# Finer steps in the last tile of two output projections, and the placing of the norms' sums and broadcasts

## The chip, the cores and the metric

The kernel runs on one core of one Trainium2 chip. The metric is the device time of one execution in microseconds (us), as the median of several runs. One execution was profiled; all rows shown here come from that one.

## The reference

Two layers of a decoder trunk are run for 1024 prompt tokens and 8 sample tokens, 1032 columns in all. Each layer normalises the residual, runs its mixer, adds the mixer's output projection to the residual, and then adds an embedding that is gated by a second normalised copy of the residual:

```python
for i in range(DEPTH):                       # DEPTH = 2
    hn = rmsnorm(h, norm_mix[i])
    if i % N_MIXERS == 0:
        y, S = hgrn2_mixer(hn, s_hgrn[j], w_in_a[j], lbs[j], gnorm_a[j], w_out_a[j])
    else:
        y, vt = chunk_mlp_mixer(hn, w_in_b[j], ln_v_g[j], ln_v_b[j], w_spatial[j], b_spatial[j], w_out_b[j])
    h = h + y                                # the output projection is the last step of the mixer
    gate = jax.nn.sigmoid(rmsnorm(h, norm_ple[i]) @ w_ple_gate[i])
    h = h + gate * (p[i] @ w_ple_proj[i])
```

The change concerns the place where `h = h + y` ends and `rmsnorm(h, norm_ple[i]) @ w_ple_gate[i]` begins. It is passed twice, once in each layer.

## The kernel before

Features lie on the 128 partitions, tokens along the free axis. The 1032 tokens are cut into three column groups c = 0, 1, 2 of 384, 384 and 264. The 1024 features of the residual are eight row tiles m = 0 to 7 (`hr[c][m]`, printed as h). Every matrix product is done as three products of split halves, high by high, high by low, low by high (`mm3`, lines 219 to 221), so a weight tile exists as whi (ScalarE's copy, line 146) and wlo (VectorE's difference, line 147), and an activation as bh and bl in the same way (lines 214 and 215; bl of odd k on VectorE, of even k on GpSimd).

`out_phase` is an output projection. For each row tile m it runs over the column groups; each takes 16 steps of k, so 48 products, and then `add` adds the result to h and squares it for the norm's sum (`ssq`, `sql`). For m = 7 `add` calls `done(c)`, which starts the norm of column group c as a generator (`norm_proc`).

A norm of a column group has these parts: its sum over the partitions on TensorE (`pss`, line 269: products with one column), `rms_e` on VectorE (line 272), the power -0.5 on GpSimd (`rsq`, line 228), the broadcast back over the partitions on TensorE (`pbc`, line 280), and then for each of eight k: `tmp` on VectorE (line 293), bh on ScalarE, bl on VectorE or GpSimd.

After m = 7 comes `ple`, the gate's projection. Its first `pair` runs two row tiles, g0 and g1, side by side: g0 of column group 0, g1 of column group 0, g0 of column group 1, and so on, each 24 products of a normalised column group with that tile's weights. So each of g0 and g1 has its own whi and wlo, split ahead of use, and at most two weight tiles are held at a time.

The order on TensorE is the order in which the program is written out. What runs beside the main loop is placed by `Ticks`: a spawned generator is resumed at a later tick, and `norm_proc` waits `d[0]` ticks before its sum and `d[1]` ticks before its broadcast. A generator takes its first step at the tick after it was spawned. The delays of both output projections' norms are in `NDEL[0]`, one pair for each column group. Before the change a tick falls after every 12 products, in `out_half` (at k % 4 == 3) and in `proj` (at k == 3 and at the end of a group). The other engines' queues are ordered by a scheduler from the instructions' priorities and the place at which they were written; once the order is fixed each engine takes its queue from front to back.

Of the kernel before, what the change touches and what calls it, by code (L numbers as in the profile page):

```python
# [19 lines left out]
KT = D // P  # L20
# [16 lines left out]
DL = 4  # L37
KB = 1
SDEL = ((6, 3), (6, 2), (4, 2))
NDEL = (((1, 2), (1, 3), (2, 2)), ((2, 2), (2, 4), (3, 3)))  # L40
OFF = (0, 384, 768)
W = (384, 384, 264)
NT = (3, 3, 2)
# [37 lines left out]
def trunk_kernel(ctx, tc, xT, st, pT, nrm, wina, lbl, gna, wouta, winb, lng, lnb, lngr, lnbr,  # L81
# [7 lines left out]
    def pool(stack, name, bufs=1, **kw):  # L89
        return stack.enter_context(tc.tile_pool(name=name, bufs=bufs, reuse_waits="tile", **kw))  # L90
# [71 lines left out]
    def load(n, wait=False):  # L162
        if n >= len(order) or n in loaded or wait and order[n][0] == "B":
            return
        if order[n][0] == "B":
            loaded[n] = load_unit(order[n][1])
            return
        if n not in staged:
            fetch_weights(n)
        stg = staged.pop(n)  # L170
        with tc.high_priority(offset=PRI if order[n][:2] == ("p", 1) or order[n][0] == "b" else 0):
            loaded[n] = split_weights(stg, 1024, PLAIN, wp)
# [29 lines left out]
    def take(*key):  # L202
        n = taken[0]
        assert order[n] == key, (order[n], key)
        load(n)
        load(n + 1, key[0] == "b")
        taken[0] += 1
        return loaded[n]


    last, rest = {}, {}

    def split(hi, lo, src, eng=V):
        last["split"] = A.copy(hi, src)  # L214
        last["lo"] = eng.tensor_tensor(lo, src, hi.bitcast(F32), ALU.subtract)  # L215

    def mm3(ps, wh, wl, xh, xl, first, last, more=False):

        PE.matmul(ps, wh, xh, start=first, stop=False, skip_group_check=more)  # L219
        PE.matmul(ps, wh, xl, start=False, stop=False, skip_group_check=more)  # L220
        PE.matmul(ps, wl, xh, start=False, stop=last, skip_group_check=more)  # L221

    def blk(t, j):
        return t[:, j * P:(j + 1) * P]
# [73 lines left out]
    def proj(wt, xh, xl, c):  # L298

        wh, wl = wt  # L300
        ps = pp.tile([P, 512], F32, name="ps_proj", tag="mm", bufs=3)
        for k in range(KT):
            mm3(ps[:, :W[c]], blk(wh, k), blk(wl, k), xh[:, k, :], xl[:, k, :], k == 0, k == KT - 1)
            if k == 3:
                tk.tick()
        return ps

# [64 lines left out]
    def stage2(tp, bufs):  # L372
        return lambda w: tp.tile([P, 2, 384], F32, name="zstg", bufs=bufs)[:, :, :w]

    def one(tile):
        return lambda w: tile()[:, :w].rearrange("p (k t) -> p k t", k=1)
# [5 lines left out]
    def out_half(ps, wt, zt, c, hf):  # L382
        for k in range(8):
            k0 = max(q for cc, q in zt if cc == c and q <= 8 * hf + k)
            zh, zl = (x[:, 8 * hf + k - k0, :] for x in zt[c, k0][:2])
            mm3(ps[:, :W[c]], blk(wt[0], k), blk(wt[1], k), zh, zl,
                hf == 0 and k == 0, hf == 1 and k == 7)
            if k % 4 == 3:
                yield 2

    def new_zt():
# [475 lines left out]
    def out_phase(key, zt, ssq, first, done, pre, parts, late, fill=None):  # L867

        with ExitStack() as s:
            st = stage2(pool(s, "zstg"), 3)  # L870
            zp = pool(s, "oz")

            def load_h(m):
                if m < KT:
                    src = xT[:, m] if first else hd[m]
                    with tc.issue_after(last["zt"].ins):
                        for c in CH:
                            nc.sync.dma_start(hr[c][m], src[:, OFF[c]:OFF[c] + W[c]])

            for c, k0, nk in parts:  # L880
                zt[c, k0] = (zp.tile([P, nk, W[c]], F32R, name=f"zh{c}_{k0}"),
                             zp.tile([P, nk, W[c]], F32R, name=f"zl{c}_{k0}"), nk)
            if fill:

                to = itertools.cycle([hr[c][m] for c in (2, 0) for m in range(4)])
                more = load_zt(zt, late[0], one(lambda: next(to)), 1, 8)
                todo = load_zt(zt, late[1], st, 2, 3)
                for gen, n in ((more, 8), (todo, 3)):
                    for _ in range(n):
                        next(gen)  # L890
                for _ in fill:
                    tk.tick()
                for _ in range(8):
                    next(more)
                run(todo)
                run(more)
            else:
                run(load_zt(zt, late, st, tie=False))
            for m in range(4):
                load_h(m)  # L900

            def bank():
                return pp.tile([P, 512], F32, name="ps_o", tag="mm", bufs=3)

            def half(ps, wt, c, hf):
                for _ in out_half(ps, wt, zt, c, hf):
                    tk.tick()

            def add(m, c, ps):
                with tc.high_priority(offset=PRI if m == KT - 1 else 0):  # L910
                    V.tensor_tensor(hr[c][m], hr[c][m], ps[:, :W[c]], ALU.add)  # L911
                accum_sq(sp, ssq[c], hr[c][m], m == 0, m == KT - 1, W[c])
                if m == KT - 1:
                    done(c)


            wt = pre["w"] if pre else take(key, 0, 0)
            for c in CH:
                if c not in pre:
                    pre[c] = bank()  # L920
                    half(pre[c], wt, c, 0)
            wt = take(key, 1, 0)
            pre1 = [pp.tile([P, 384], F32, name="ps_o1", tag=t, bufs=1) for t in ("pA", "po", "pt")]
            for c in CH:
                half(pre1[c], wt, c, 0)
            for m, pm in ((0, pre), (1, pre1)):
                wt = take(key, m, 1)
                for c in CH:
                    half(pm[c], wt, c, 1)
                    add(m, c, pm[c])  # L930
            for m in range(2, KT):
                wts = [take(key, m, hf) for hf in range(2)]
                load_h(m + 2)
                for c in CH:
                    ps = bank()
                    for hf in range(2):
                        half(ps, wts[hf], c, hf)
                    add(m, c, ps)

    def ple(l, ep, hh, hl, ssq, done, mid=None):  # L940
        def group(m, c, wg, pj):
            w = W[c]
            pg = proj(wg, hh[c], hl[c], c)
            gt = sp.tile([P, 384], F32, name="tmp", bufs=4)
            with tc.high_priority(offset=PRI if m >= KT - 2 else 0):
                A.activation(gt[:, :w], pg[:, :w], AF.Sigmoid)
                V.tensor_tensor(gt[:, :w], gt[:, :w], pj[:, OFF[c]:OFF[c] + w], ALU.mult)
                V.tensor_tensor(hr[c][m], hr[c][m], gt[:, :w], ALU.add)
            accum_sq(sp, ssq[c], hr[c][m], m == 0, m == KT - 1, w)
            if l == 0:  # L950
                nc.sync.dma_start(hd[m][:, OFF[c]:OFF[c] + w], hr[c][m])
            tk.tick()

        def start(m):
            pj = ep.tile([P, T], F32, name="pj", bufs=2)
            nc.sync.dma_start(pj, ppd[l][m])
            return take("g", l, m), pj

        def pair(m):
            a, b = start(m), start(m + 1)  # L960
            for c in CH:
                group(m, c, *a)
                group(m + 1, c, *b)
                if m == KT - 2:
                    done(c)

        pair(0)
        for m in range(2, KT - 2):
            if m == 3 and mid:
                mid()  # L970
            a = start(m)
            for c in CH:
                group(m, c, *a)
        pair(KT - 2)

    def norm_spawn(c, ssq, gi, act, d):
# [3 lines left out]
    act = new_act()  # L980
    out_phase("oa", zt, ssq, True, lambda c: norm_spawn(c, ssq, 1, act, NDEL[0]), pre,
              [(c, 8, 8) for c in CH], [(c, 8) for c in CH])
# [35 lines left out]
    with ExitStack() as sG:  # L1018
# [3 lines left out]
        with ExitStack() as s:  # L1022
# [7 lines left out]

            ple(0, ep, act[0], act[1], ssq2, lambda c: tk.spawn(norm_rows(c, ssq2, 2, hn, NDEL[1][c])), mid)
            for i, _ in enumerate(pple(1, ph, pl, 0, places([(pq, "pple_t", 8)]))):
# [250 lines left out]
    for g in range(8):  # L1283
# [15 lines left out]
        else:  # L1299
# [17 lines left out]
            def first():  # L1317
# [8 lines left out]
    act3 = new_act()  # L1326
    out_phase("ob", zt, ssq3, False, lambda c: norm_spawn(c, ssq3, 3, act3, NDEL[0]), {},
              [(1, 12, 4), (2, 0, 8)], [[(2, 0), (2, 8)], [(0, 8), (1, 8), (1, 12)]], pple(1, ph, pl, 1, lambda c, mm: hr[c][4 + mm]))
# [106 lines left out]
```

## Time and profile before

| | |
|---|---|
| median of 3 runs | 1916.89 us (1912.62, 1916.89, 1918.22) |
| the profiled execution | 1914.28 us, of which 1912.4 us from first to last instruction |
| TensorE (PE) busy | 1882.9 us, 98% of the span |
| VectorE (DVE) busy | 1156.3 us, 60% |
| ScalarE (ACT) busy | 800.1 us, 42% |
| GpSimd (POOL) busy | 432.8 us, 23% |
| mean granted TensorE clock | 0.993 of full speed |

In rows of a timeline the first number is the start in us from the span's beginning, the second the duration, then engine, line, operation, tiles (out<-in), shape and count. Durations of products overlap, since they are pipelined; the distance from start to start tells the pace. A bracket names the engine's idle time just before and what ended it. The first output projection ends near 948 us, the second near 1802 us.

### The profile page before, as it was taken

Reading aid. Unit: us, or ns where it says so; the run is one execution under the profiler, and the core shown is the slowest. Engines: PE = TensorE matmul, PEld = TensorE weight load, DVE = VectorE, ACT = ScalarE, POOL = GpSimd, SP = SyncE. Lnnn points to the kernel's source line nnn. Section 1 sums busy time; section 2 is a strip of 40 time slices with the busy share of each in tenths; the row PEclk is TensorE's granted clock in tenths of the full one; section 3 lists DMA queues with packets and bytes.
Section 4 is the critical chain, followed back from the end, with each engine's and each line's share of the span. In section 5 each row is a group of like instructions: output and inputs, shape, how many; then the busy total and the mean of one; then the engine's idle time right before and its main releaser. Section 6 shows DMA issues by size and latency. Waiting matters only on the chain.

```text
span 1912.4 us, 33713 instructions
## 1 busy us (share of the span) xinstructions
PE 1882.9 (98%) x13250; PEld 1856.2 (97%) x13250; DVE 1156.3 (60%) x2610; ACT 800.1 (42%) x1711; POOL 432.8 (23%) x441
## 2 busy tenths in 40 slices
PE   9999999999999999999999999999999999999997
PEld 8999999999999998999999999999999999999997
DVE  5967676766767677411465755577777776311455
ACT  6463544444454546311244544434434335311342
POOL 4110000000010001011233332345445451011321
PEclk8999999999999999999999999999999999999998
DMA  6231323222231326711243343323333236611123
GB/s 214 76 117 61 118 72 103 78 81 78 92 99 60 111 69 191 251 49 51 76 143 117 109 145 99 90 81 106 124 114 106 97 108 197 222 45 45 67 89 111
DMA packets 124302, 203.76 MB, mean 107 GB/s; under 512 B 11568, under 2 KB 97264, under 8 KB 123120
## 3 DMA queue, kind: packets, MB, share of 16 engines
q1 hardware_dynamic: 124144, 201.61, 32.2%
q8 instruction: 104, 1.70, 0.4%
q14 instruction: 54, 0.44, 0.1%
HBM read 148.75 MB, written 52.82 MB: 105 GB/s over the span
## 4 chain that ended last, share of the span: by engine, by line
PE 90%; DVE 5%; DMA 2%; POOL 1%; ACT 1%; issue 1%; SPq 0%; DVEq 0%; ACTq 0%; POOLq 0%
PE ps_proj L219 18%; PE ps_proj L221 18%; PE ps_proj L220 18%; PE ps_o L219 6%; PE ps_o L220 6%; PE ps_o L221 6%; PE ps_d L221 1%; PE ps_d L219 1%; PE ps_d L220 1%; PE psp L1255 1%; PE pC L672 1%; PE pt_o L718 1%; PE p L638 1%; PE pt_g L1061 1%; PE pss L269 1%
## 5 line engine op out<-in xcount | busy, mean ns | idle before, releaser
L219 PE MATMUL ps_proj<-bh,whi 128*128 128x384 f32 (+1 forms) x2160 | 695.1, 322 | 2.1 <-ACT pple_t L338 1.6
L221 PE MATMUL ps_proj<-bh,wlo 128*128 128x384 f32 (+1 forms) x2160 | 679.9, 315 | 0.5 <-DVE wlo L147 0.5
L220 PE MATMUL ps_proj<-bl,whi 128*128 128x384 f32 (+1 forms) x2160 | 678.8, 314 | 1.4 <-POOL bl L215 1.4
L219 PEld LDWEIGHTS ps_proj<-bh,whi 128*128 128x128 f32 x2160 | 407.4, 189 | 3.6 <-ACT pple_t L338 1.7
L220 PEld LDWEIGHTS ps_proj<-bl,whi 128*128 128x128 f32 x2160 | 407.8, 189 | 2.6 <-POOL bl L215 2.6
L221 PEld LDWEIGHTS ps_proj<-bh,wlo 128*128 128x128 f32 x2160 | 406.5, 188 | 1.7 <-DVE wlo L147 1.7
L147 DVE TENSOR_TENSOR wlo<-wstg,whi 128x1024 fp32r<-128x1024 f32 x148 | 184.8, 1249 | 147.4 <-ACT whi L146 146.2
L146 ACT CAST whi<-wstg 128x1024 fp32r<-128x1024 f32 x148 | 155.0, 1048 | 155.2 <-PE ps_proj L220 104.1
L255 POOL TENSOR_TENSOR ssq<-ssq,tmp 128x384 f32<-128x384 f32 (+1 forms) x72 | 76.3, 1060 | 406.7 <-ACT tmp L254 359.9
L911 DVE TENSOR_TENSOR h<-h,ps_o 128x384 f32<-128x384 f32 (+1 forms) x48 | 24.6, 512 | 192.4 <-PE ps_o L221 190.9
L254 ACT ACTIVATE tmp<-h 128x384 f32<-128x384 f32 (+1 forms) x72 | 35.3, 491 | 219.3 <-DVE h L911 168.9
L219 PE MATMUL ps_o<-bh,whi 128*128 128x384 f32 (+1 forms) x384 | 122.1, 318 | 0.0
L220 PE MATMUL ps_o<-bl,whi 128*128 128x384 f32 (+1 forms) x384 | 121.8, 317 | 0.0
L221 PE MATMUL ps_o<-bh,wlo 128*128 128x384 f32 (+1 forms) x384 | 121.8, 317 | 0.0
L146 ACT CAST shi<-ssum 128x512 fp32r<-128x512 f32 x88 | 54.6, 622 | 110.0 <-PE ps_proj L220 60.2
L219 PE MATMUL ps_o<-zh,whi 128*128 128x384 f32 (+1 forms) x288 | 90.1, 313 | 0.0
L220 PE MATMUL ps_o<-zl,whi 128*128 128x384 f32 (+1 forms) x288 | 89.7, 312 | 0.0
L221 PE MATMUL ps_o<-zh,wlo 128*128 128x384 f32 (+1 forms) x288 | 89.7, 312 | 0.0
L215 POOL TENSOR_TENSOR ql<-q,qh 128x384 fp32r<-128x384 f32 (+1 forms) x24 | 22.4, 931 | 254.5 <-ACT qh L214 254.5
L147 DVE TENSOR_TENSOR slo<-ssum,shi 128x512 fp32r<-128x512 f32 x88 | 68.8, 783 | 12.0 <-ACT shi L146 12.0
L675 DVE TENSOR_TENSOR q<-q,t 128x192 f32<-128x192 f32 (+1 forms) x144 | 47.4, 330 | 44.7 <-PE pC L672 38.3
L219 PEld LDWEIGHTS ps_o<-bh,whi 128*128 128x128 f32 x384 | 72.2, 188 | 0.0
(303 smaller groups left out, 3930.5 us busy)
## 6 DMA issues: line engine op xcount, KB each, us to landing
wstg<-in_wina SPq DMA_DIRECT2D x48, 512.0 KB, 3.7
wstg<-in_winb SPq DMA_DIRECT2D x48, 512.0 KB, 3.7
pj<-ppd SPq DMA_DIRECT2D x16, 516.0 KB, 5.2
S<-in_st SPq DMA_DIRECT2D x16, 512.0 KB, 5.4
vb<-vd SPq DMA_DIRECT2D x16, 512.0 KB, 4.6
out_so_s<-S SPq DMA_DIRECT2D x16, 512.0 KB, 3.4
wstg<-in_wouta SPq DMA_DIRECT2D x16, 512.0 KB, 3.5
wstg<-in_wgate SPq DMA_DIRECT2D x16, 512.0 KB, 3.5
```

The lines of the kernel that those rows point to most:

```text
L146: A.copy(hi, src)
L147: V.tensor_tensor(lo, src, hi.bitcast(F32), ALU.subtract)
L215: last["lo"] = eng.tensor_tensor(lo, src, hi.bitcast(F32), ALU.subtract)
L219: PE.matmul(ps, wh, xh, start=first, stop=False, skip_group_check=more)
L220: PE.matmul(ps, wh, xl, start=False, stop=False, skip_group_check=more)
L221: PE.matmul(ps, wl, xh, start=False, stop=last, skip_group_check=more)
L254: A.activation(sq[:, :w], src, AF.Square)
L255: eng.tensor_tensor(ssq, ssq, sq[:, :w], ALU.add)
L269: PE.matmul(pss[:, i:i + 1], t[:, o:o + P], ones[:, 0:1], start=j == 0, stop=j == len(parts) - 1)
L638: PE.matmul(blk(p0, i), blk(Y, i), blk(X, i), start=True, stop=True)
L675: V.tensor_tensor(ql[:, :, 1, :], ql[:, :, 1, :], t2[:, :, 0:1].broadcast_to([P, n, lv]), ALU.mult)
L911: V.tensor_tensor(hr[c][m], hr[c][m], ps[:, :W[c]], ALU.add)
```

## The change

Within the last row tile (m = 7) of both output projections and in the first pair of the gate's projection, a tick falls after every 6 products instead of 12; elsewhere ticks stay. The delays of the norms that start there are given in the finer ticks, and are other numbers.

```diff
-NDEL = (((1, 2), (1, 3), (2, 2)), ((2, 2), (2, 4), (3, 3)))
+NDEL = (((3, 2), (4, 3), (3, 3)), ((2, 2), (2, 4), (3, 3)))
...
+    fine = [False]
+
...
-            if k == 3:
+            if k == 3 or fine[0] and k in (1, 5):
                 tk.tick()
...
-            if k % 4 == 3:
+            if k % 4 == 3 or fine[0] and k % 2:
                 yield 2
...
             for m in range(2, KT):
                 wts = [take(key, m, hf) for hf in range(2)]
+                fine[0] = m == KT - 1
                 load_h(m + 2)
...
         pair(0)
+        fine[0] = False
```

Counted in products on TensorE, the places become these. "Into c=1" means after so many products of that column group's 48 in row tile m = 7; "into the pair" after so many products of the gate's first pair.

| norm of | sum before | sum now | broadcast before | broadcast now |
|---|---|---|---|---|
| c=0 | 24 into c=1 | 24 into c=1 | 48 into c=1 | 36 into c=1 |
| c=1 | 24 into c=2 | 30 into c=2 | 12 into the pair | 48 into c=2 |
| c=2 | 36 into the pair | 24 into the pair | 60 into the pair | 42 into the pair |

No instruction of TensorE, ScalarE or GpSimd is added or removed. The numbers behind names below tell buffers apart; lines of the changed kernel are two or three higher than those of the kernel before.

On TensorE, first output projection, the sum of c=2 and the products around it. Before, it stands inside the group of g1 and column group 0 (ps_proj_11741, weights whi_11662 and wlo_11663):

```order
L221 MATMUL ps_proj_11741<-bh0_10185,wlo_11663 128x384
L269 MATMUL pss_11754<-ones_71,ssq2_10184 128x1
L269 MATMUL pss_11754<-ones_71,sql_11630 128x1
L269 MATMUL pss_11754<-ones_71,ssq2_10184 128x1
L269 MATMUL pss_11754<-ones_71,sql_11630 128x1
L269 MATMUL pss_11754<-ones_71,ssq2_10184 128x1
L269 MATMUL pss_11754<-ones_71,sql_11630 128x1
L219 MATMUL ps_proj_11741<-bh0_10185,whi_11662 128x384
```

In the changed kernel it stands between the group of g0 (ps_proj_11710) and that of g1 (ps_proj_11752, weights whi_11698 and wlo_11699):

```order
L223 MATMUL ps_proj_11710<-bh0_10185,wlo_11419 128x384
L271 MATMUL pss_11741<-ones_71,ssq2_10184 128x1
L271 MATMUL pss_11741<-ones_71,sql_11666 128x1
L271 MATMUL pss_11741<-ones_71,ssq2_10184 128x1
L271 MATMUL pss_11741<-ones_71,sql_11666 128x1
L271 MATMUL pss_11741<-ones_71,ssq2_10184 128x1
L271 MATMUL pss_11741<-ones_71,sql_11666 128x1
L221 MATMUL ps_proj_11752<-bh0_10185,whi_11698 128x384
L222 MATMUL ps_proj_11752<-bl0_10188,whi_11698 128x384
L223 MATMUL ps_proj_11752<-bh0_10185,wlo_11699 128x384
```

The sum has moved 12 products forward, from the middle of g1's first group to just ahead of its first product; the third product after it is the first that reads g1's wlo.

On VectorE at the same place, the split of g1's weights and the rms_e of c=2. Before, wlo_11663 stands eight instructions ahead of rms_e_11761:

```order
L147 TENSOR_TENSOR wlo_11663<-wstg_11660,whi_11662 128x1024
L215 TENSOR_TENSOR bl0_10188<-tmp_11564,bh0_10185 128x384
L293 SCALAR_TENSOR_TENSOR tmp_11691<-h1_0_10163,g32_72,pbc_11687 128x384
L293 SCALAR_TENSOR_TENSOR tmp_11695<-h1_1_10164,g32_72,pbc_11687 128x384
L293 SCALAR_TENSOR_TENSOR tmp_11699<-h1_2_10165,g32_72,pbc_11687 128x384
L293 SCALAR_TENSOR_TENSOR tmp_11703<-h1_3_10166,g32_72,pbc_11687 128x384
L215 TENSOR_TENSOR bl1_10189<-tmp_11695,bh1_10186 128x384
L293 SCALAR_TENSOR_TENSOR tmp_11707<-h1_4_10167,g32_72,pbc_11687 128x384
L272 TENSOR_SCALAR rms_e_11761<-pss_11754 128x3
```

In the changed kernel wlo_11699 stands five instructions behind rms_e_11748:

```order
L295 SCALAR_TENSOR_TENSOR tmp_11653<-h1_5_10168,g32_72,pbc_11629 128x384
L274 TENSOR_SCALAR rms_e_11748<-pss_11741 128x3
L217 TENSOR_TENSOR bl1_10189<-tmp_11645,bh1_10186 128x384
L295 SCALAR_TENSOR_TENSOR tmp_11657<-h1_6_10169,g32_72,pbc_11629 128x384
L217 TENSOR_TENSOR bl1_10189<-tmp_11653,bh1_10186 128x384
L295 SCALAR_TENSOR_TENSOR tmp_11661<-h1_7_10170,g32_72,pbc_11629 128x384
L147 TENSOR_TENSOR wlo_11699<-wstg_11696,whi_11698 128x1024
```

The split of g1's weights has moved from ahead of the rms_e of c=2 to behind it and behind the rest of column group 1's norm.

On VectorE in the second output projection, the changed kernel has the same rows:

```order
L274 TENSOR_SCALAR rms_e_20561<-pss_20554 128x3
L217 TENSOR_TENSOR bl1_18821<-tmp_20477,bh1_18818 128x384
L295 SCALAR_TENSOR_TENSOR tmp_20489<-h1_6_18801,g32_72,pbc_20461 128x384
L217 TENSOR_TENSOR bl1_18821<-tmp_20485,bh1_18818 128x384
L295 SCALAR_TENSOR_TENSOR tmp_20493<-h1_7_18802,g32_72,pbc_20461 128x384
L147 TENSOR_TENSOR wlo_20513<-wstg_20510,whi_20512 128x1024
```

So g1's weights (wlo_20513) have moved in the same way there.

## Rows read from the trace of the kernel before

**Rows 1.** The page: span, TensorE's and the other engines' busy time, and the granted clock in 40 slices of the span (9 is full speed).

```profile
span 1912.4 us, 33713 instructions
...
PE 1882.9 (98%) x13250; PEld 1856.2 (97%) x13250; DVE 1156.3 (60%) x2610; ACT 800.1 (42%) x1711; POOL 432.8 (23%) x441
...
PEclk8999999999999999999999999999999999999998
```

**Rows 2.** The page: the chain that ended last, its share of the span by engine.

```profile
PE 90%; DVE 5%; DMA 2%; POOL 1%; ACT 1%; issue 1%; SPq 0%; DVEq 0%; ACTq 0%; POOLq 0%
```

**Rows 3.** Who TensorE waited for over the whole span, the first and the third of 17 such pairs: us in total, how often, the longest in us.

```profile
PE ps_pple L219 <- ACT h L338: 3.8, 1, 3.8
...
PE pt_o L718 <- DVE ss_e L712: 2.4, 1, 2.4
```

**Rows 4.** Timeline of TensorE in the last tile of the first output projection: the first product behind the sum of c=0, and the broadcast of c=0.

```profile
936.66 0.42 PE L219 MATMUL ps_o<-zh,whi 128*128 128x384 f32 x1
...
940.92 0.83 PE L280 MATMUL pbc<-ident,rsq 128*128 128x128 f32 x6
```

**Rows 5.** Timeline of TensorE in the gate's projection behind it: a wait for bl, the sum of c=2 and the products behind it, and a wait for the weights of the third row tile.

```profile
951.90 0.34 PE L219 MATMUL ps_proj<-bh,whi 128*128 128x384 f32 x1
952.82 0.44 PE L220 MATMUL ps_proj<-bl,whi 128*128 128x384 f32 x1 [0.58 <-POOL bl L215]
...
955.89 0.28 PE L269 MATMUL pss<-ones,ssq 128*128 128x1 f32 x2
...
957.15 0.42 PE L219 MATMUL ps_proj<-bh,whi 128*128 128x384 f32 x1
...
957.58 0.33 PE L221 MATMUL ps_proj<-bh,wlo 128*128 128x384 f32 x1
...
974.31 0.33 PE L220 MATMUL ps_proj<-bl,whi 128*128 128x384 f32 x1
975.11 0.44 PE L221 MATMUL ps_proj<-bh,wlo 128*128 128x384 f32 x1 [0.46 <-DVE wlo L147]
975.39 0.34 PE L219 MATMUL ps_proj<-bh,whi 128*128 128x384 f32 x1
```

**Rows 6.** Timeline of TensorE behind the second output projection: its wait for bl.

```profile
1806.38 0.34 PE L219 MATMUL ps_proj<-bh,whi 128*128 128x384 f32 x1
1807.58 0.45 PE L220 MATMUL ps_proj<-bl,whi 128*128 128x384 f32 x1 [0.86 <-POOL bl L215]
```

**Rows 7.** Timeline of VectorE behind the first output projection: the split of g1's weights, rms_e of c=2 and what follows it, and the split of the third row tile's weights.

```profile
950.69 1.21 DVE L147 TENSOR_TENSOR wlo<-wstg,whi 128x1024 fp32r<-128x1024 f32 x1
...
957.32 0.16 DVE L272 TENSOR_SCALAR rms_e<-pss 128x3 f32<-128x3 f32 x1 [1.04 <-PE pss L269]
957.40 0.55 DVE L215 TENSOR_TENSOR bl<-tmp,bh 128x384 fp32r<-128x384 f32 x1
957.87 1.66 DVE L293 SCALAR_TENSOR_TENSOR tmp<-h,g,pbc 128x384 f32<-128x384 f32 x3
959.44 0.62 DVE L215 TENSOR_TENSOR bl<-tmp,bh 128x384 fp32r<-128x384 f32 x1
...
973.85 1.21 DVE L147 TENSOR_TENSOR wlo<-wstg,whi 128x1024 fp32r<-128x1024 f32 x1
```

**Rows 8.** Timeline of GpSimd at the same place: rsq of c=0, and the bl (two calls run into one row) for which TensorE waits in Rows 5.

```profile
937.08 0.85 POOL L228 TENSOR_TENSOR rsq<-rms_e,mhalf 128x3 f32<-128x3 f32 x1 [10.43 <-DVE rms_e L272]
...
950.66 2.10 POOL L215 TENSOR_TENSOR bl<-tmp,bh 128x384 fp32r<-128x384 f32 x1 [2.69 <-ACT bh L214]
```

**Rows 9.** Timeline of ScalarE: the copy of the third row tile's weights.

```profile
971.84 1.06 ACT L146 CAST whi<-wstg 128x1024 fp32r<-128x1024 f32 x1
```

**Rows 10.** Stretches of the span: length, busy time and count on PE, PEld, DVE, ACT and POOL, then the granted TensorE clock, the DMA share and GB/s.

```profile
748.80:751.70 2.90, 0.58 (x6) 0.38 (x4) 1.58 (x4) 2.90 (x8) 0.00 (x0) 1.00 0.68 205
752.00:755.20 3.20, 3.20 (x13) 3.10 (x12) 2.86 (x8) 2.97 (x9) 0.37 (x1) 0.50 0.86 238
1608.00:1611.10 3.10, 0.00 (x0) 0.00 (x0) 3.10 (x8) 1.00 (x3) 0.00 (x0) 1.00 0.46 119
1612.20:1615.40 3.20, 3.20 (x12) 3.20 (x11) 0.40 (x1) 0.96 (x2) 0.00 (x0) 0.50 0.88 236
...
28.40:31.60 3.20, 2.50 (x8) 2.50 (x9) 3.20 (x4) 2.69 (x7) 2.97 (x4) 0.50 0.42 133
31.60:34.80 3.20, 3.20 (x12) 3.20 (x11) 1.94 (x5) 3.17 (x7) 2.85 (x4) 0.50 0.47 159
41.00:43.60 2.60, 2.60 (x25) 2.60 (x25) 0.52 (x1) 0.89 (x2) 0.10 (x1) 1.00 0.03 6
45.40:48.60 3.20, 3.20 (x19) 2.72 (x18) 2.23 (x4) 0.78 (x3) 1.82 (x2) 1.00 0.00 0
```

**Rows 11.** Timeline of TensorE around its longest wait: products ahead of it and behind it.

```profile
1606.80 0.34 PE L220 MATMUL ps_pple<-bl,whi 128*128 128x384 f32 x1
1606.97 0.34 PE L221 MATMUL ps_pple<-bh,wlo 128*128 128x384 f32 x1
1611.15 0.44 PE L219 MATMUL ps_pple<-bh,whi 128*128 128x384 f32 x1 [3.84 <-ACT h L338]
...
1612.41 0.52 PE L219 MATMUL ps_pple<-bh,whi 128*128 128x384 f32 x1
1612.73 0.52 PE L220 MATMUL ps_pple<-bl,whi 128*128 128x384 f32 x1
```

## The prediction

> **What bounds the kernel.** I read the page first. TensorE is busy for 98% of the span and the chain that ended last lies on it for 90% [rows 1, 2]; its clock is at full speed in all but the first and last slice as shown. So what counts is what TensorE does in the two changed places, and only that: a microsecond of waiting put in or taken out there is a microsecond of the span, and there are just two such places.
>
> Then I read TensorE's timeline there, for gaps between starts that exceed the usual pace. A product of 384 columns follows the one before after 0.17 us [rows 11]. Three gaps stand out. Behind the first output projection a product waits for bl: 951.90 to 952.82 is 0.92 instead of 0.17 [rows 5]. Some 22 us later the third product of the third row tile waits for its wlo, 0.80 instead of 0.17 [rows 5]. Behind the second output projection there is the same wait for bl, 1.20 instead of 0.17 [rows 6], and none for wlo. After a wait the next product follows after 0.28 instead of 0.17 (975.11 to 975.39 [rows 5]), 0.11 more. So the waits cost 0.75 + 0.11 = 0.86, 0.63 + 0.11 = 0.74 and 1.03 + 0.11 = 1.14, together 2.7 us. This is all that better placing can win: 0.14% of the span. Each sum and broadcast also breaks the run of products, but their number stays.
>
> **The moved sums and broadcasts themselves.** The broadcast of c=0 moves forward by 12 products. Its place comes at 936.66 + 0.09 + 12 x 0.17 = 938.8 instead of 940.92 [rows 4]; rsq is there at 937.08 + 0.85 = 937.9 [rows 8], so it does not wait. The norm of c=0 starts 2.1 us earlier, on a VectorE, ScalarE and GpSimd that have room there, while the first group of the pair starts a little later, since the broadcast of c=1 now stands ahead of it. The bl that ended at 950.66 + 2.10 = 952.8 [rows 8] is then in time for its product, which comes due at about the same 951.90 + 0.17 = 952.1 as before; VectorE's own bl gains alike. I take both waits for bl as gone: -0.86 and -1.14. The wait for the third tile's wlo: its whi can be copied only when the fifth group has let go of the buffer. In the trace ScalarE began at 971.84 [rows 9] and VectorE split at 973.85 [rows 7], after other work. In the changed kernel everything on TensorE there is later by some 2.3 us (the 3.2 below less 0.86) and VectorE is ahead with the norm of c=2, so the split follows its copy at once and ends, by the durations 1.06 and 1.21, about half a microsecond ahead of the product: -0.74. If it is not gone, the sum rises by that.
>
> **The split that is now late.** This is the term that decides. The split of g1's weights moved on VectorE's queue from ahead of rms_e of c=2 to behind it, in both places, as the orders show. rms_e reads the sum of c=2, and TensorE makes this sum directly ahead of g1's first product. VectorE takes its queue from front to back, so wlo of g1 cannot begin before the sum is done, and g1's third product needs it. Before, that split ran at 950.69, more than 6 us ahead of rms_e at 957.32 [rows 7].
>
> Price it from the end of the sum, 957.15 in the trace [rows 5]. rms_e starts 0.17 later at 957.32, the next bl 0.08 later at 957.40, and what follows that bl 0.47 later at 957.87 [rows 7]. A tmp takes (959.44 - 957.87) / 3 = 0.52 [rows 7]. So: 0.17 + 0.08 + bl 0.47 + tmp 0.52 + bl 0.47 + tmp 0.52 + wlo 1.21 = 3.44. The product starts 0.05 behind its wlo (973.85 + 1.21 = 975.06 to 975.11 [rows 5, 7]): 3.49 after the sum. Without a wait it is due 957.58 - 957.15 = 0.43 after the sum [rows 5]. The wait is 3.06, with the slower restart 3.2 us, twice: +6.3. Bounds: with the bl of 0.47 and the tmp of 0.52 each as short as shown it cannot fall much under 2.9; if both bl stretch like the 0.62 at 959.44 [rows 7] and tmp waits for a buffer, 3.7. Behind the waiting product stand all of TensorE's products, so nothing hides it. Sum so far: 6.3 - 2.7 = +3.6 us.
>
> The other queues: on the sync engine's DMA queue the fourth gate tile's load now waits for this later split, and is wanted only when the pair and the third tile are through; on ScalarE the gate's sigmoid of g1, c=0 falls behind six bh of c=2, with three banks to write to before its own is wanted. Both at nothing; if that cover failed it would show as a wait of a later group.
>
> **The clock after the wait.** A wait of this size may cost more than itself. After the longest wait of the trace (3.8 us [rows 3], nothing on TensorE from 1608.00 to 1611.10) the granted clock stood at 0.50, the 1.2 GHz level, from 1612.20 to 1615.40 [rows 10]; after the 2.4 us wait [rows 3] that lies in 748.80 to 751.70 it stood at 0.50 from 752.00 to 755.20 [rows 10]. At 0.50 products follow after 0.32 instead of 0.17 [rows 11]: 3.2 us hold 10 of them, which costs 10 x 0.15 = 1.5 us. Here the 3.1 us of waiting come just after 1.3 us of one-column sums (955.89 to 957.15 [rows 5]), with only 0.4 us of full products between, so I take one such stretch behind each wait: +3.0. The lower bound is 0: 2.6 us of such sums at 41.00 passed without a change (1.00 at 45.40 [rows 10]), though no wait followed there. The upper one is a double stretch, as the 0.50 in both 28.40 to 31.60 and 31.60 to 34.80 [rows 10], behind sums and a wait at the start: +3.0 each.
>
> The Trainium skill speaks against this term: "TensorE: Matmul & The Clock Gate", section "HAM oscillation — how this bites in real kernels", names a length of idle time as the one to stay under, and the wait forecast here stays under it. By that rule the clock would stay and the sum would be +3.6. The row of the 2.4 us wait, shorter still and followed by 0.50, does not agree with it, so I go by the row.
>
> **Sum.** 6.3 - 2.7 + 3.0 = +6.6 us, 0.34%. Against the profiled execution's own 1914.28 (1912.4 span and 1.9 around it) this is 1920.9. The profiled execution lies 2.6 under the median of the runs; the changed kernel's time will be a median too, so I put the 6.6 on 1916.89: **1923.5 us**.
>
> **The rivals.**
> (a) The forecast: wait of 3.1 in both places, one stretch at half clock behind each, +6.6. Chance 0.52.
> (b) The same waits, and the clock lowered more: double stretches, +3.0 each, or one double and longer waits: +8 to +12.6, say 1926 to 1929. For it: the 28.40 case, and that sums, two products and a wait follow each other here. Chance 0.20.
> (c) The waits, and the clock holds in both places or in one: +3.6 to +5.1, 1920.5 to 1922. For it the case at 41.00; the rule named above ends here too. Chance 0.20.
> (d) Not slower: the split of g1's weights is done in time, so only the three old waits go: -2.7, 1914.2. This would need VectorE to pass rms_e, two bl, two tmp and wlo within 0.43 us of the sum's end; it decides at a chain of 0.43 against the 3.49 that the rows give, or the sum of c=2 to end 3 us before g1's first product, which the order on TensorE excludes. Chance 0.08, mostly for something in the queues that I misread.
>
> **How the numbers follow.** About 0.3%, 5.7 us, is what a measurement of this kernel can tell from no change. (b) lies beyond it, (a) 0.9 us beyond it, so that the scatter of runs (1912.6 to 1918.2) takes back about a sixth of it: slower 0.20 + 0.43 + a little of (c) = 0.65. Same: the rest of (a), nearly all of (c), most of (d): 0.31. Faster 0.04. The range leaves out (d) and the far end of (b) and adds some scatter at both ends: 1917.5 to 1929.5. The likeliest case alone: 1921 to 1926.
>
> **What would show it.** In the changed kernel's trace: a third product of g1's first group with a wait of about 3.1 us for wlo, some 6 to 10 us behind the end of each output projection; VectorE's wlo there starting 2.1 us after rms_e, which starts 0.2 after the last one-column sum; no wait for bl in the first group; no wait for the third tile's wlo; a granted clock of 0.50 for 3 us within a few us of each wait, with products 0.32 apart. It would be wrong if wlo stood ready, if the wait were far from 3, or if the clock stayed at 1.00 (then 1920.5) or fell for longer.

## The result, and the profile after

The changed kernel takes 1924.82 us (1920.91 to 1927.27), the kernel before 1915.07 us (1912.62 to 1918.22) on the same chip, 7 runs each. The ratio is 1.0048, interval 1.0039 to 1.0057: the change costs 9.2 us (7.5 to 10.9). A second comparison of the same two kernels gave 1.0031 (1.0019 to 1.0044), so 5.9 us (3.6 to 8.4). What both allow is 7.5 to 8.4 us. One execution of a kernel below, that with 18 spare products, took 7245 us and is left out of its ratio.

The page of the changed kernel answers to [rows 1]. The profiled execution took 1927.27 us, 12.8 us more in span.

```profile
span 1925.2 us, 33708 instructions
...
PE 1889.0 (98%) x13250; PEld 1863.6 (97%) x13250; DVE 1159.0 (60%) x2610; ACT 800.7 (42%) x1711; POOL 432.7 (22%) x441
```

TensorE has the same 13250 products and is busy 6.1 us longer. Products that are not more but take longer point to the clock; what else the span has gained is waiting. On what TensorE waited, the list of its waits says (us in total, times, longest):

```profile
PE ps_proj L223 <- DVE wlo L147: 6.4, 2, 3.2
```

A wait for wlo, twice 3.2 us, has come to the head of the list, ahead of what led it before [rows 3], and no wait for bl is left in it. TensorE's timeline, first in the first layer and then in the second, answers to [rows 4 to 6]:

```profile
939.87 0.42 PE L221 MATMUL ps_o<-zh,whi 128*128 128x384 f32 x1
...
952.22 0.33 PE L222 MATMUL ps_proj<-bl,whi 128*128 128x384 f32 x1
...
957.48 0.42 PE L221 MATMUL ps_proj<-bh,whi 128*128 128x384 f32 x1
957.74 0.34 PE L222 MATMUL ps_proj<-bl,whi 128*128 128x384 f32 x1
961.26 0.69 PE L223 MATMUL ps_proj<-bh,wlo 128*128 128x384 f32 x1 [3.18 <-DVE wlo L147]
...
1816.93 0.34 PE L222 MATMUL ps_proj<-bl,whi 128*128 128x384 f32 x1
1820.45 0.69 PE L223 MATMUL ps_proj<-bh,wlo 128*128 128x384 f32 x1 [3.19 <-DVE wlo L147]
1820.94 0.52 PE L221 MATMUL ps_proj<-bh,whi 128*128 128x384 f32 x1
1821.26 0.52 PE L222 MATMUL ps_proj<-bl,whi 128*128 128x384 f32 x1
```

The first bl (952.22) bears no bracket: its wait is gone. The third product of g1's first group waits: 957.74 to 961.26 is 3.52, 3.35 more than the usual 0.17, and the same in the second layer. Behind it products follow after 0.32 (1820.94 to 1821.26), so the clock is down. One row shows something else: the product behind the sum of c=0 starts at 939.87, in the trace of before at 936.66 [rows 4]. So 3.2 of the 12.8 us were lost before the changed code was reached. That belongs to this one execution, not to the change: in a second profile of the changed kernel the same product starts earlier than in the trace of before.

```profile
935.07 0.42 PE L221 MATMUL ps_o<-zh,whi 128*128 128x384 f32 x1
```

The stretches at half clock (columns as in [rows 10]):

```profile
961.20:964.40 3.20, 3.14 (x10) 3.14 (x11) 2.32 (x4) 0.52 (x1) 0.87 (x1) 0.50 0.45 164
1818.00:1824.60 6.60, 4.15 (x13) 4.15 (x14) 4.70 (x6) 1.94 (x4) 3.25 (x3) 0.50 0.26 79
```

TensorE worked 3.14 and 4.15 us at 0.50; in the second place the clock was down from 1818.00 on, while TensorE still waited. As products come after 0.32 instead of 0.17, such a microsecond loses 0.15 / 0.32 = 0.47: 1.5 and 1.9 us, together 3.4.

Last, VectorE around the wait, which answers to [rows 7]:

```profile
952.31 0.62 DVE L295 SCALAR_TENSOR_TENSOR tmp<-h,g,pbc 128x384 f32<-128x384 f32 x1 [0.38 <-PE pbc L282]
953.20 0.61 DVE L295 SCALAR_TENSOR_TENSOR tmp<-h,g,pbc 128x384 f32<-128x384 f32 x1 [0.27 <-POOL bl L217]
...
956.01 1.65 DVE L295 SCALAR_TENSOR_TENSOR tmp<-h,g,pbc 128x384 f32<-128x384 f32 x3
957.66 0.16 DVE L274 TENSOR_SCALAR rms_e<-pss 128x3 f32<-128x3 f32 x1
957.74 0.55 DVE L217 TENSOR_TENSOR bl<-tmp,bh 128x384 fp32r<-128x384 f32 x1
...
958.73 0.82 DVE L217 TENSOR_TENSOR bl<-tmp,bh 128x384 fp32r<-128x384 f32 x1
959.47 0.60 DVE L295 SCALAR_TENSOR_TENSOR tmp<-h,g,pbc 128x384 f32<-128x384 f32 x1
960.00 1.21 DVE L147 TENSOR_TENSOR wlo<-wstg,whi 128x1024 fp32r<-128x1024 f32 x1
```

rms_e starts 0.18 us behind the sum (957.66, against 957.48 when TensorE went on), just as forecast. But it bears no bracket. VectorE was not idle before it; it had only then finished three tmp of c=1. In the trace of before rms_e did wait, 1.04 [rows 7]. So VectorE is late by its own work. From the first tmp of c=1 at 952.31 to the end of wlo at 961.21 its only pause in the trace is the 0.27 us ahead of the second tmp, and all eight tmp of c=1 stand ahead of the split. ScalarE's half of that split was done long before:

```profile
951.39 1.05 ACT L146 CAST whi<-wstg 128x1024 fp32r<-128x1024 f32 x1 [1.30 <-PE ps_o L222]
```

So from 952.44 on it is VectorE's queue that keeps wlo back, as far as the trace shows; the experiments test it.

### The profile page after: what moved, and what is told of

It reads as the page before. It is cut to its first block, busy times and chain, and to the rows that moved or that the text cites. A ratio compares the mean times of both kernels' runs of the same rounds, so it can differ in the third digit from the quotient of the medians.

```text
span 1925.2 us, 33708 instructions
## 1 busy us (share of the span) xinstructions
PE 1889.0 (98%) x13250; PEld 1863.6 (97%) x13250; DVE 1159.0 (60%) x2610; ACT 800.7 (42%) x1711; POOL 432.7 (22%) x441
## 4 chain that ended last, share of the span: by engine, by line
PE 90%; DVE 5%; DMA 2%; POOL 1%; ACT 1%; issue 1%; SPq 0%; DVEq 0%; ACTq 0%; POOLq 0%
PE ps_proj L221 18%; PE ps_proj L223 18%; PE ps_proj L222 18%; PE ps_o L221 6%; PE ps_o L222 6%; PE ps_o L223 6%; PE ps_d L223 1%; PE ps_d L221 1%; PE ps_d L222 1%; PE psp L1259 1%; PE pC L674 1%; PE pt_o L720 1%; PE p L640 1%; PE pss L271 1%; PE pt_g L1065 1%
## 5 line engine op out<-in xcount | busy, mean ns | idle before, releaser
L222 PEld LDWEIGHTS ps_o<-bl,whi 128*128 128x128 f32 x384 | 72.2, 188 | 0.0
```

## The experiments

Two theories. S, the one on record: wlo waits for the sum of c=2 because it stands behind rms_e. B: wlo waits for the norm of c=1, all of which stands ahead of it on VectorE since its broadcast was moved into c=2, where it is written before the weights of g1 are asked for. And on the clock: do the waits bring the half speed, and what does it cost? Edits are against the changed kernel; ratios are against the kernel before on the same chip. Where the text says that an instruction stands ahead of another or behind it, VectorE's queue is meant, if no other engine is named.

**The sum of c=2 put back.** 36 into the pair, its broadcast at 60, as before the change; all else as changed. rms_e then stands behind the split.

```diff
-NDEL = (((3, 2), (4, 3), (3, 3)), ...
+NDEL = (((3, 2), (4, 3), (5, 4)), ...
```

> The change with the sum and broadcast of c=2 put back to 36 and 60 products into the pair; c=0 and c=1 as changed. On VectorE the split of g1's weights keeps its place behind the eight tmp of c=1, but rms_e of c=2 now comes after it. Theory S (the recorded one: the split waits for the sum of c=2): the wait for wlo of g1 is gone, and with the old waits gone too the time is 2.7 us under the kernel before. Theory B (the split is late because the whole norm of c=1 stands ahead of it, since the broadcast of c=1 is now written before the pair's weights are called for; the sum has no part in it): VectorE's split ends within 0.2 us of where it did, the group of g1 begins 1.3 us earlier because the sums no longer stand ahead of it, so the wait grows from 3.2 to about 4.4 us in both places, and with the clock lowered behind it the time is 9 to 12 us over the kernel before.

Measured: 1929.34 us, ratio 1.0076 (1.0061 to 1.0092), +14.5 us. TensorE's and VectorE's timelines and the half-clock stretches:

```profile
953.30 0.34 PE L222 MATMUL ps_proj<-bl,whi 128*128 128x384 f32 x1
958.31 0.69 PE L223 MATMUL ps_proj<-bh,wlo 128*128 128x384 f32 x1 [4.67 <-DVE wlo L147]
```
```profile
949.21 0.61 DVE L295 SCALAR_TENSOR_TENSOR tmp<-h,g,pbc 128x384 f32<-128x384 f32 x1 [0.38 <-PE pbc L282]
...
956.75 1.50 DVE L147 TENSOR_TENSOR wlo<-wstg,whi 128x1024 fp32r<-128x1024 f32 x1
...
964.27 0.16 DVE L274 TENSOR_SCALAR rms_e<-pss 128x3 f32<-128x3 f32 x1 [4.48 <-PE pss L271]
```
```profile
957.40:967.40 10.00, 9.09 (x32) 9.09 (x33) 2.51 (x5) 0.52 (x1) 0.85 (x1) 0.50 0.20 72
1817.40:1831.00 13.60, 11.46 (x40) 11.46 (x41) 4.56 (x9) 1.84 (x4) 1.84 (x2) 0.50 0.12 39
```

rms_e now starts 7.5 us after the split, and the wait is longer, not gone. S falls. B holds in kind; the wait and the time are both beyond what it gave (4.4, and 9 to 12 us). The split still begins 956.75 - 949.21 = 7.5 us after the first tmp of c=1, against 960.00 - 952.31 = 7.7 in the changed kernel: rms_e had cost it 0.15. What grew is mainly TensorE's lead, since the six one-column sums (1.25 us) no longer stand ahead of g1's first product; the split itself also took 1.50 instead of 1.21. The longer waits are followed by 9.1 and 11.5 us of work at half clock, some 9.7 us lost (x 0.47). With two waits of 5.01 - 0.17 = 4.84, 0.11 each for the restart and the old waits' -2.7 that makes +16.9, within the interval's 17.6.

**The broadcast of c=1 put back.** 12 into the pair, as before; the sum of c=2 stays where the change put it.

```diff
+NDEL = (((3, 2), (4, 5), (3, 3)), ...
```

> The change with only the broadcast of c=1 put back to 12 products into the pair (its sum at 30 into c=2 as changed); c=0 and c=2 as changed. On VectorE the split of g1's weights then stands ahead of all tmp of c=1. Theory S (the sum of c=2 directly ahead of g1's group is the cause): a wait for wlo of g1 stays near 3 us, the time 6 to 10 us over the kernel before. Theory B (the place of the broadcast of c=1 is the cause): no wait for wlo of g1, the two old waits for bl gone as well, no clock stretch at 0.50 behind the two places, and the time 2 to 3 us under the kernel before.

Measured: 1912.44 us, ratio 0.9993 (0.9983 to 1.0003), -1.3 us (-3.3 to +0.6). VectorE's timeline and the granted clock over both places:

```profile
949.28 1.80 DVE L147 TENSOR_TENSOR wlo<-wstg,whi 128x1024 fp32r<-128x1024 f32 x1 [0.53 <-ACT whi L146]
...
951.48 2.18 DVE L295 SCALAR_TENSOR_TENSOR tmp<-h,g,pbc 128x384 f32<-128x384 f32 x4
954.44 0.16 DVE L274 TENSOR_SCALAR rms_e<-pss 128x3 f32<-128x3 f32 x1 [0.79 <-PE pss L271]
```
```profile
940.00:990.00 50.00, 50.00 (x336) 49.88 (x335) 40.48 (x68) 26.66 (x53) 20.72 (x20) 1.00 0.43 146
1796.00:1840.00 44.00, 44.00 (x301) 44.00 (x300) 32.49 (x58) 22.25 (x45) 18.07 (x18) 1.00 0.20 73
```

The split stands ahead of the four tmp again and waits for ScalarE's whi alone. TensorE is busy for the whole of both stretches, at full clock. Put back, this one number takes the wait away. B holds.

**The split put first, by priority.** All places as changed; the split of g1's weights alone is given a high priority, so that the scheduler puts it ahead of c=1's norm.

```diff
-        with tc.high_priority(offset=PRI if order[n][:2] == ("p", 1) or order[n][0] == "b" else 0):
+        early = order[n][0] == "g" and order[n][2] == 1
+        with tc.high_priority(offset=PRI if order[n][:2] == ("p", 1) or order[n][0] == "b" or early else 0):
```

> The change with every sum and broadcast where it puts them, and only the split of g1's weights in both layers raised in the scheduler's priority, so that on VectorE it stands behind the first tmp of c=1 instead of behind all eight. Theory S: rms_e of c=2 is now behind the split, so no wait, 2 to 3 us under the kernel before. Theory B: the same. If instead the wait came from something that both miss (the copy whi on ScalarE, the load), a wait for wlo of 1 us or more stays. A new wait for bl of column group 0 or 1 of up to 1 us is possible, since the split now stands ahead of their norms.

Measured: 1911.75 us, ratio 0.9990 (0.9981 to 0.9998), -1.9 us. VectorE, then TensorE at the third row tile:

```profile
945.94 0.61 DVE L296 SCALAR_TENSOR_TENSOR tmp<-h,g,pbc 128x384 f32<-128x384 f32 x1 [0.38 <-PE pbc L283]
946.47 1.42 DVE L147 TENSOR_TENSOR wlo<-wstg,whi 128x1024 fp32r<-128x1024 f32 x1
...
951.27 0.16 DVE L275 TENSOR_SCALAR rms_e<-pss 128x3 f32<-128x3 f32 x1
```
```profile
970.42 0.34 PE L223 MATMUL ps_proj<-bl,whi 128*128 128x384 f32 x1
971.40 0.44 PE L224 MATMUL ps_proj<-bh,wlo 128*128 128x384 f32 x1 [0.64 <-DVE wlo L147]
```

The split comes behind one tmp instead of eight and the wait is gone, with all sums and broadcasts where the change put them. The wait for the third tile's wlo, however, is here again (0.98 - 0.17 = 0.81).

**Only the broadcast of c=0 moved.** Sums and broadcasts of c=1 and c=2 as before.

```diff
+NDEL = (((3, 2), (3, 6), (5, 4)), ...
```

> Finer steps kept, but only the broadcast of c=0 is moved (36 into c=1); sums and broadcasts of c=1 and c=2 stand where they stood before. On VectorE the split of g1's weights then stands ahead of the tmp of c=1 again. If the cause is the broadcast of c=1 (written ahead of the split): no wait for g1's wlo, the waits for bl gone, no 0.50 at either place, -2 us (-4 to 0) against the kernel before, so within 0.3%. If any earlier norm makes the split late (a rival: VectorE is simply too full once c=0's norm moves), a wait of 1 to 3 us for wlo stays and the time is 3 to 8 us above the kernel before.

Measured: 1911.38 us, ratio 0.9987 (0.9978 to 0.9996), -2.5 us (-4.2 to -0.8). VectorE, and TensorE over both places:

```profile
949.92 1.22 DVE L147 TENSOR_TENSOR wlo<-wstg,whi 128x1024 fp32r<-128x1024 f32 x1
...
951.78 2.19 DVE L295 SCALAR_TENSOR_TENSOR tmp<-h,g,pbc 128x384 f32<-128x384 f32 x4 [0.16 <-PE pbc L282]
```
```profile
940.00:990.00 50.00, 50.00 (x337) 49.96 (x336) 39.50 (x67) 27.33 (x53) 20.35 (x20) 1.00 0.42 142
1796.00:1840.00 44.00, 44.00 (x295) 43.98 (x295) 31.79 (x57) 22.07 (x44) 17.06 (x17) 1.00 0.21 74
```

No gap is left in either place: the three old waits are gone. So the earlier norm of c=0 brings all that the change can win here, and the -2.7 of the prediction is about what it is worth. Neither this kernel nor the two above beats the kernel before by more than 0.3%.

**The wait filled with work, wholly.** 18 spare products of 384 columns behind the sum of c=2, in both places.

```diff
+NBUSY = 18
...
+        def keep_busy(wg):
+            pd_ = pp.tile([P, 512], F32, name="spare", tag="pA", bufs=1)
+            for k in range(NBUSY):
+                PE.matmul(pd_[:, :384], blk(wg[0], k % 8), hh[0][:, k % 8, :], start=k == 0, stop=k == NBUSY - 1)
...
+                if fine[0] and c == 0:
+                    keep_busy(a[0])
```

> The change as it is, plus 18 spare products of 384 columns into an unused bank between the sum of c=2 and g1's first group, in both layers (3.1 us at full clock); they are read by nothing and fill the time in which TensorE otherwise waits for wlo. If the loss beyond the two waits is the lowered clock: the granted clock stays at 1.00 in both places, the wait for wlo shrinks to under 0.4 us, and the time falls 3 to 5 us under the change, to about 4 us over the kernel before. If the clock had no part: the time equals that of the change, 9 to 10 us over the kernel before.

Measured: 1918.73 us, ratio 1.0021 (1.0012 to 1.0029), +4.0 us (2.3 to 5.6). The granted clock over both places:

```profile
954.00:966.00 12.00, 11.91 (x73) 11.59 (x74) 10.59 (x21) 5.67 (x13) 7.27 (x7) 1.00 0.40 135
1810.00:1822.00 12.00, 11.90 (x70) 11.59 (x70) 10.59 (x22) 5.80 (x15) 6.76 (x7) 1.00 0.14 45
```

The wlo comes no sooner, but TensorE is not idle meanwhile and the clock stays at 1.00. So the half speed of the changed kernel is brought by the waits.

**Half filled, beside the changed kernel once more.** 8 spare products instead of 18 (`NBUSY = 8`), and the changed kernel unaltered on the same chip.

> The changed kernel with 8 spare products of 384 columns behind the sum of c=2 in each of the two places (added work, its result is read by nothing): 8 x 0.17 = 1.4 us of what was a 3.2 us wait is filled, about 1.8 us of waiting is left. The wait itself ends when it did, so without the clock the time is that of the changed kernel. Theory that the length of the wait sets the clock: the shorter wait is no longer followed by 0.50 and the time is that of the kernel with 18 spare products, +4 us against the kernel before. Theory that any wait behind the sums lowers it: 0.50 for one stretch at each place, +7 us. Theory that the clock has nothing to do with the remaining 5 us: as the changed kernel, +9 us, with 1.00 behind the waits.

> The changed kernel once more, beside the two kernels below on one chip. Both theories: +9 us (+7.5 to +10.9), ratio 1.004 to 1.0057; a wait of 3.2 us for the wlo of g1 in both places and a granted clock of 0.50 behind each. Read here: whether the stretches at 0.50 behind the two waits are single or double again, and whether half-clock stretches elsewhere in the span differ from the first profiled execution, as they should if those are scatter.

Measured: 1918.41 us, ratio 1.0022 (1.0011 to 1.0034), +4.2 us with 8 spare products; 1921.0 us, 1.0031 (1.0019 to 1.0044), +5.9 us for the changed kernel. With 8 spare products the waits and what followed the second are these, TensorE's timeline and the clock:

```profile
957.74 0.45 PE L224 MATMUL ps_proj<-bh,wlo 128*128 128x384 f32 x1 [1.83 <-DVE wlo L148]
958.02 0.34 PE L222 MATMUL ps_proj<-bh,whi 128*128 128x384 f32 x1
...
1813.79 0.48 PE L224 MATMUL ps_proj<-bh,wlo 128*128 128x384 f32 x1 [1.83 <-DVE wlo L148]
1814.07 0.52 PE L222 MATMUL ps_proj<-bh,whi 128*128 128x384 f32 x1
```
```profile
954.00:962.00 8.00, 6.17 (x37) 5.85 (x37) 6.59 (x12) 2.67 (x7) 4.34 (x3) 1.00 0.46 157
1814.20:1817.40 3.20, 3.20 (x12) 3.20 (x11) 1.83 (x3) 0.52 (x1) 0.40 (x1) 0.50 0.53 164
```

The same wait of 1.83 us was followed by full speed in one place and by 0.50 in the other. None of the three theories put for 8 spare products is met in both places: one place kept the clock, the other had one stretch at half. By time this kernel can't be told from the changed one on that chip, as the intervals overlap. The changed kernel's own +5.9 (3.6 to 8.4) lies below the +9 expected of it; the two intervals share 7.5 to 8.4. The granted clock of the changed kernel, in its second profile:

```profile
955.00:961.60 6.60, 5.15 (x16) 5.16 (x17) 3.69 (x5) 1.04 (x2) 2.25 (x2) 0.50 0.33 112
1815.20:1818.40 3.20, 3.20 (x10) 3.20 (x11) 2.16 (x3) 0.53 (x1) 0.72 (x1) 0.50 0.52 164
```

Its waits are 3.19 us in both places, as before, but here the first place has the longer stretch and the second the shorter. In the first place it begins while TensorE still waits. The lost time is (5.15 + 3.20) x 0.47 = 3.9 us, against 3.4 in the first profile. Elsewhere in the span the half-clock stretches differ too, as expected of scatter: from 20 to 50 us the mean granted clock was 0.79 in the first profile and 0.89 in the second.

## Why the prediction was right, and where it was not

**Direction and size: right, the size with some luck.** 1923.5 was forecast, 1924.82 measured, and the likeliest case, a late split with the clock down behind it, is what the trace shows. The base of the forecast, the median of three runs (1916.89), was 1.8 us above the median of seven (1915.07). As a difference +6.6 was forecast and +9.2 measured, below the interval of the first comparison (7.5 to 10.9) and inside that of the second (3.6 to 8.4).

**The three waits that go: right.** Both waits for bl are gone (952.22, with no bracket), and so is the third tile's wait for wlo, for the list of waits holds only the two new ones. The kernel with only c=0 moved shows the value: -2.5 measured for -2.7. That the third tile's wait returns when the split is put first (0.81) fits the prediction's reason, that it goes because TensorE is later there; with only c=0 moved, and with the broadcast of c=1 put back, it is gone without such a delay, so that reason is not the whole one; what else takes it away stays open.

**The size of the wait: a little short.** Forecast 3.06, and 3.2 with the restart; measured 3.35, which with the restart of 0.11 is 3.46. The chain from rms_e to the split, forecast at 0.08 + 2 x (0.47 + 0.52) = 2.06, took 960.00 - 957.66 = 2.34, mostly because the second bl took 0.74 from start to start. That lies within the bounds (2.9 to 3.7). Two waits are +6.9 instead of +6.3.

**The step that failed** is the sentence in "The split that is now late" that wlo "cannot begin before the sum is done". In the queue it is true; as the cause it is wrong. VectorE reached rms_e at 957.66 by its own backlog, by chance just as the sum's result was there, so the price worked out from the sum's end came out nearly right. It did so in both layers, as both engines set out from the same broadcast of c=1 and had about equally much to do. The kernel with the sum put back shows it: no rms_e ahead, a split only 0.15 us sooner after the first tmp, and a wait of 4.67. The rows to price were those of VectorE from the broadcast of c=1 on: first tmp to the end of wlo 961.21 - 952.31 = 8.9 us, while TensorE needed wlo at 957.91, 5.6 us after that tmp. The order on VectorE that the front part shows, with wlo also behind the rest of c=1's norm, had this in it. Rival (d) took its condition from the same mistake: it asked for a sum that ends 3 us earlier, but a split with no sum ahead of it was hardly sooner, while a broadcast of c=1 that comes later took the wait away.

**The clock: right in kind, short in size.** One stretch behind each wait was forecast, 3.0 us in all. The two profiles of the changed kernel show one of 3.2 us and one of 6.6 us each, and 3.4 and 3.9 us lost. This is half of rival (b): a double stretch in one place of two. All four of these waits of 3.2 us came with 0.50, and so did one of the two of 1.83, so the row of the 2.4 us wait was a good guide. The kernels in which the wait was gone or wholly filled kept 1.00 there.

The Trainium skill's page that was weighed, "TensorE: Matmul & The Clock Gate", section "HAM oscillation — how this bites in real kernels", names a length of idle time to stay under, and by it the clock would have stayed up behind these waits. The trace does not agree (0.50 behind 3.2 us).

For the lower bound of this term the prediction named the sums at 41.00 that passed without a change. The same trace has the other case: one-column products fill TensorE from 14.90 to 17.40, no wait follows, and the clock falls all the same.

```profile
14.90:17.40 2.50, 2.50 (x25) 2.50 (x23) 0.88 (x2) 1.37 (x3) 0.00 (x0) 1.00 1.06 382
18.20:21.40 3.20, 3.20 (x13) 3.20 (x12) 0.00 (x0) 1.51 (x3) 2.39 (x3) 0.50 1.08 358
```

So the 1.25 us of sums ahead of the wait may have a part in the half clock here. The kernel with 18 spare products has the same sums and kept 1.00, so they do not bring it alone; how much they add to the wait no run tells.

**The sum with measured terms:** 6.9 - 2.7 + 3.4 = 7.6 by the first profile, 8.1 by the second, where 6.6 was forecast. Both lie in what the two comparisons allow, 7.5 to 8.4. The kernel with 18 spare products fits too: its third product starts 3.81 us after the sum (954.97 to 958.78) instead of 0.43, so 2 x (3.38 + 0.11) - 2.7 = +4.3 for 4.0 measured.

```profile
954.97 3.37 PE L948 MATMUL spare<-bh,whi 128*128 128x384 f32 x18
...
958.78 0.44 PE L224 MATMUL ps_proj<-bh,wlo 128*128 128x384 f32 x1
```

The traces also show the cost of the two places by itself, free of what the rest of the span adds. Take the time from the product behind the sum of c=0 to the fourth product of the third row tile, in each layer. In the trace of before this is 936.66 to 975.39 [rows 4, 5] and 1791.15 to 1829.59; in the first profile of the changed kernel 939.87 to 982.03 and 1799.07 to 1841.67. Against before, in us:

| kernel | first layer | second layer | both |
|---|---|---|---|
| changed, first profile | +3.43 | +4.16 | +7.6 |
| changed, second profile | +4.30 | +3.76 | +8.1 |
| sum of c=2 put back | +7.66 | +9.03 | +16.7 |
| broadcast of c=1 put back | -1.48 | -1.26 | -2.7 |
| split put first | -0.54 | -1.23 | -1.8 |
| only c=0 moved | -1.50 | -1.23 | -2.7 |
| 18 spare products | +1.96 | +2.28 | +4.2 |
| 8 spare products | +1.97 | +3.80 | +5.8 |

Each sum lies within the interval that was measured for its kernel, and each sum worked out above (7.6, 8.1, +16.9, -2.7, +4.3) is met within 0.2 us. With 8 spare products the waits are equal; less what the old waits are worth there (-1.50 and -1.23), the two places are 1.6 us apart, and that is the clock (3.20 x 0.47 = 1.5). Of the first profile's 12.8 us, 7.6 are the change; 3.2 were lost ahead of it and 2.0 elsewhere in the span.

## What to carry to other kernels

When a step is written earlier, look at everything that it releases on the other engines' queues, and at what was written behind it: here eight tmp came ahead of a split that could have run 7 us sooner. If a late instruction stands behind several others, look for the idle bracket: an instruction that bears none did not hold the queue up by any amount that the trace shows, however neatly its time fits. Then take it away, and see whether the wait goes. Here a wait of 3.2 us on a busy TensorE cost about half as much again in clock, and one of 4.7 us about as much again. So the placing that wins as much with the fewest moves (here only c=0 moved) is the one to keep.

## What the runs showed of the hardware

A wait of 1.83 us between full products was followed by 0.50 of the clock in one place and by 1.00 in the other of the same execution. With waits of 3.2 us the stretch at 0.50 was 3.2 or 6.6 us, and which place got the longer one changed from one execution to the next. With waits of 4.7 us it was 10.0 and 13.6 us. The longer stretches began before the wait had ended. So the price of one wait is not fixed: 1.5 to 2.4 us for 3.2 us of waiting here. What decides between these cases no run shows.
